# Hybrid decoder trunk: how the weight pairs of the feed-forward block are brought in, and how its output tiles are added to the residual

## The chip, the cores and the metric

The kernel runs on one core of one Trainium2 chip. The metric is device time in microseconds (us) for one execution. The five engines are TensorE (PE for its matmuls, PEld for its weight loads), VectorE (DVE), ScalarE (ACT), GpSimd (POOL) and SyncE (SP). Transfers are issued by an engine's queue in the order of that engine's program and carried out by 16 DMA engines that all queues share. An instruction whose input is not there holds up everything behind it on its own engine.

## The reference, cut to what matters

Two layers over 512 tokens with a width of 1024. Each layer has three token mixers (attention in a window, a short convolution, a state space model), merged by gates, and then a feed-forward block with a hidden width of 2816; a final RMSNorm ends it. The change touches the feed-forward block only:

```
h = rmsnorm(x, norm_ffn[i])
gt, up = jnp.split(h @ w_ffn_in[i], 2, axis=-1)
x = x + (jax.nn.silu(gt) * up) @ w_ffn_out[i]
```

Everything is float32. A float32 product is made of three matmuls on split operands: each operand is a high part `h` (the value rounded to fp32r) and a low part `l` (the value less `h`), and the product is hh + lh + hl.

## The kernel before, in words

**Tiles.** Activations lie transposed, 128 channels by 512 tokens to a tile. A weight chunk is fetched as a raw tile, ACT copies it to `h` with rounding (`A.copy`), DVE subtracts to get `l` (`lo_of`), and PE uses both.

**The pairs.** The hidden width is cut into 22 tiles of 128, in the groups 0-5, 6-9, 10-13, 14-17 and 18-21. The first six tiles are plain. From tile 6 on, the gate tile and the up tile of a hidden tile make a *pair*, which is computed with seven products of half-sized blocks in place of eight (`seven_products`). A pair item needs the four blocks a11, a12, a21, a22 of its weights, two sums of them and a copy of one, each split into `h` and `l`. The groups 6-9, 10-13 and 14-17 are also multiplied by the output weights in this way (`out_pairs`): two pair items for each group, each used for four of the eight output tiles. Their results are added to the residual, which is kept in DRAM in `xkept`. A layer has 22 pair items: 16 for hidden tiles and 6 for out pairs. The out pairs of a group come behind the first hidden tile of the next group, so the items are, from 0: tiles 6, 7, 8, 9, 10, then out pairs (items 5 and 6), tiles 11 to 14, out pairs (11 and 12), tiles 15 to 18, out pairs (17 and 18), tiles 19 to 21. This stretch is called the pair stretch below. Group 18-21 is multiplied out plainly at its end (`pfo`).

**How a pair item is brought in.** `fetch_chunk` issues for each item, on POOL's queue: r2 = (a21, a11) (L175); h4 = a22, rounded to fp32r by the transfer (L176); then (a22, a21) accumulated onto r2 by a transfer (L177), which has to wait until the first load of r2 has landed; and r1 = (a11, a12) (L178). `item_steps` then lets ACT write -h4 into l4 (L195) and a transfer on POOL's queue accumulate a22 onto it (L196). DVE makes r3 from r2 and r1 (L225, L227); ACT makes h1, h2, h3 (L223, L230, L234) and DVE l1, l2, l3 (L190).

**How an output tile is stored.** For each pair of output tiles `out_pairs` loads both residual tiles from `xkept` ahead (L1184, tiles `xs`), adds the products on DVE and stores each tile back (L1189, L1193), all on SP's queue.

**What sets the order.** The program is traced in the order of the code and then put into an order for each engine by a scheduler that works on a timeline of its own. Buffers are handed out in that order: r1, r2 and r3 share 5 buffers, `h` and `l` of weights have 5 each, and 58 buffers of 128x512 (pool `u2`) hold all the rest, h4, l4, `xs`, ga and ub among them. A transfer or an operation that writes a buffer waits until the last use of its previous content is over.

Of the kernel before, what the change touches and what calls it, by code (L numbers as in the profile page):

```python
# [9 lines left out]
F32 = mybir.dt.float32  # L10
F32R = mybir.dt.float32r
I32 = mybir.dt.int32
AF = mybir.ActivationFunctionType
ALU = mybir.AluOpType
PSUM = bass.MemoryType.PSUM

P = 128
D = 1024
S = 512
DEPTH = 2  # L20
KT = D // P
# [59 lines left out]
def hybrid_kernel(ctx, tc, xin, wst, wsp, vec, ssp, ssb, sbt, cst, out):  # L81
    nc = tc.nc
    V, A, T = nc.vector, nc.scalar, nc.tensor
# [13 lines left out]
    def u2(shape, dt=F32, name="u2"):  # L97
        return up.tile(shape, dt, tag="u2", bufs=NU2, name=name)
# [58 lines left out]
    raws = []  # L157

    def wraw(name, dt=F32):
        return wp.tile([P, 1024], dt, tag="part", bufs=NPART, name=name)  # L160

    def whi(name="whi", dt=F32R):
        return wp.tile([P, 1024], dt, tag="whi", bufs=NHI, name=name)

    def wlo(name="wlo", dt=F32R):
        return wp.tile([P, 1024], dt, tag="wlo", bufs=NLO, name=name)

    def fetch_chunk(queue=nc.sync, parts=1):
        i, n, *half = items[loaded[0]]
        loaded[0] += 1  # L170
        if n is None:

            r1, r2, h4 = wraw("r1"), wraw("r2"), u2([P, S], F32R, "h4")
            n = half[0]
            nc.gpsimd.dma_start(r2[:, : 2 * n], wsp[i, :, 1024 : 1024 + 2 * n])  # L175
            nc.gpsimd.dma_start(h4[:, :n], wsp[i, :, 2048 : 2048 + n])  # L176
            nc.gpsimd.dma_start(r2[:, : 2 * n], wsp[i, :, 2048 : 2048 + 2 * n], accum_op=ALU.add)  # L177
            nc.gpsimd.dma_start(r1[:, : 2 * n], wsp[i, :, 0 : 2 * n])  # L178
            raws.append((i, n, r1, r2, h4))
            return None  # L180
        raw = wp.tile([P, 1024], F32, tag="raw", bufs=NRAW, name="raw")
        n //= parts
        cuts = [slice(j * n, (j + 1) * n) for j in range(parts)]
        for c in cuts:
            dma = queue.dma_start(raw[:, c], wst[i, :, c])
        raws.append((raw, cuts))
        return dma

    def lo_of(lo, raw, hi):
        V.tensor_tensor(out=lo, in0=raw, in1=hi.bitcast(F32), op=ALU.subtract)  # L190
        return lo

    def rest_of(lo, hi, src):

        A.activation(lo, hi.bitcast(F32), AF.Copy, scale=-1.0)  # L195
        nc.gpsimd.dma_start(lo, src, accum_op=ALU.add)  # L196
        return lo

    fetched = [0]
# [1 line left out]
    def item_steps():  # L201
        if not raws:
            fetch_chunk()
        got = raws.pop(0)
        while sum(1 + (len(x) > 3) for x in raws) < fetched[0] and loaded[0] < len(items):
            fetch_chunk()
        if len(got) == 2:
            raw, cuts = got
            hi, lo = whi(), wlo()
            for c in cuts:  # L210
                A.copy(hi[:, c], raw[:, c])  # L211
                yield
                lo_of(lo[:, c], raw[:, c], hi[:, c])
                yield
            ready.append((cuts[-1].stop * 3 // P, (hi, lo)))
            return
        i, n, r1, r2, h4 = got
        a, b, ab = slice(0, n), slice(n, 2 * n), slice(0, 2 * n)
        l4 = u2([P, S], F32R, "l4")
        rest_of(l4[:, a], h4[:, a], wsp[i, :, 2048 : 2048 + n])  # L220
        yield
        h1 = whi("h1")
        A.copy(h1[:, ab], r1[:, ab])  # L223
        r3 = wraw("r3")
        V.tensor_tensor(out=r3[:, a], in0=r2[:, a], in1=r1[:, a], op=ALU.add)  # L225
        yield
        V.tensor_tensor(out=r3[:, b], in0=r3[:, a], in1=r1[:, b], op=ALU.add)  # L227
        yield
        h2, l1 = whi("h2"), wlo("l1")
        A.copy(h2[:, ab], r2[:, ab])  # L230
        lo_of(l1[:, ab], r1[:, ab], h1[:, ab])
        yield
        h3, l2 = whi("h3"), wlo("l2")
        A.copy(h3[:, ab], r3[:, ab])  # L234
        lo_of(l2[:, ab], r2[:, ab], h2[:, ab])
        yield
        l3 = wlo("l3")
        lo_of(l3[:, ab], r3[:, ab], h3[:, ab])
        part = lambda h, l, c: (h[:, c], l[:, c])
        ready.append((7 * n // P * 3 // 2,  # L240
            dict(a11=part(h1, l1, a), a12=part(h1, l1, b), s1=part(h2, l2, a), s3=part(h2, l2, b),
                 s2=part(h3, l3, a), s4=part(h3, l3, b), a22=part(h4, l4, a))
        ))
        yield

    def load_chunk():
        for _ in item_steps():
            pass
# [3 lines left out]
    def feed(steps=1000):  # L252

        while steps and sum(n for n, _ in ready) < AHEAD and (feeding or raws or loaded[0] < len(items)):
            if not feeding:
                feeding.append(item_steps())
            if next(feeding[0], "end") == "end":
                feeding.pop()
            steps -= 1

    def take():
        while not ready:
            feed(1)
        return ready.pop(0)[1]
# [97 lines left out]
    def tt(out, a, b, op):  # L362
        V.tensor_tensor(out=out, in0=a, in1=b, op=op)
        return out

    def stt(out, a, s, b, o0, o1):
        V.scalar_tensor_tensor(out=out, in0=a, scalar=s, in1=b, op0=o0, op1=o1)
        return out
# [10 lines left out]
    for k in range(KT):  # L379
# [3 lines left out]
        if k == 3:  # L383
            fetch_chunk()
    xg = []
    first = item_steps()
    with tc.manual_schedule(engines={mybir.EngineType.DVE, mybir.EngineType.Activation}):
        for k in range(KT):
# [63 lines left out]
    def first_products(ssum):  # L452

        u = u_products(ssum)
        pq, ws = [mmps([P, S], "pqb") for _ in range(NB - 1)], [chunk()]
        q_products(pq, ws, [0], range(NB - 1))
        u = u_evacuated(*u)
        ws.append(chunk())
        q_products(pq, ws, [1], range(NB - 1))
        pq.append(mmps([P, S], "pqb"))  # L460
        q_products(pq, ws, [0, 1], [NB - 1])
        return u + ((pq, ws),)
# [5 lines left out]
    uts, rcol, rb, r2, qprod = first_products(ssum)  # L468
# [16 lines left out]
    def tiny(dt=F32, shape=(P, LQ)):  # L485
        _n[0] += 1
        return cp.tile(list(shape), dt, name=f"ssm_c{_n[0]}")
# [73 lines left out]
    for lo_, hi_, by in ((2, 3, 1), (3, 5, 2)):  # L561
        n = hi_ - lo_
        dst = [pw[:, i, lo_:hi_] for i in range(2)]
        src = [pw[:, i, lo_ - by : hi_ - by] for i in range(2)]
        m = [pw[:, i, by : by + 1].to_broadcast([P, n, LQ]) for i in range(2)]
# [27 lines left out]
    r4 = er  # L593
    for _ in range(2):
        cph, sph = double_angle(cph, sph)
        r4 = tt(tiny(), r4, r4, ALU.mult)
# [324 lines left out]
    for l in range(DEPTH):  # L921
        if l > 0:
            uts, rcol, rb, r2, qprod = first_products(ssum)
# [204 lines left out]
        flat = lambda x: x.rearrange("p a c -> p (a c)")  # L1128
# [34 lines left out]
        def pair_tile(made, beside):  # L1163

            ga, ub, pd, pb = seven_products(ops, beside, take())

            def evacuated():
                tt(ga, ga, pd, ALU.add)
                A.activation(ga, ga, AF.Silu)
                yield  # L1170
                stt(ub, pb, -1.0, ub, ALU.mult, ALU.subtract)
                yield
                yield from made(flat(ga), flat(ub))

            return [evacuated()]

        def out_pairs(ops, beside):

            xs = []

            def fetch_x(m):
                xs.append([u2([P, S], F32, "xs") for _ in range(2)])
                for j in range(2):
                    nc.sync.dma_start(xs[-1][j], xkept[:, m + j])  # L1184

            def evacuated(m, x, ga, ub, pd, pb):
                tt(ga, ga, pd, ALU.add)
                tt(x[0], x[0], flat(ga), ALU.add)
                nc.sync.dma_start(xkept[:, m], x[0])  # L1189
                yield  # L1190
                stt(ub, pb, -1.0, ub, ALU.mult, ALU.subtract)
                tt(x[1], x[1], flat(ub), ALU.add)
                nc.sync.dma_start(xkept[:, m + 1], x[1])  # L1193
                yield

            fetch_x(0)
            for m in range(0, KT, 2):
                if m + 2 < KT:
                    fetch_x(m + 2)
                if m % 4 == 0:  # L1200
                    w = take()
                got = seven_products(ops, beside, w, m % 4)
                beside = [evacuated(m, xs.pop(0), *got)]
            return beside

        xkept = dr.tile([P, KT, S], F32, name=f"xkept{l}")
        nonlocal_rb = []
        beside, due = [], []
        for gi, (f0, f1) in enumerate(FGROUPS):
# [14 lines left out]
            for f in range(f0, f1):  # L1224
# [12 lines left out]
                beside = pair_tile(made, beside)  # L1237
                if due:
                    beside = out_pairs(due.pop(), beside)
# [6 lines left out]
            beside = []  # L1246
# [238 lines left out]
```

## Time and profile before

| | |
|---|---|
| time, median of 3 runs | 1584.59 us (1581.96 to 1584.94) |
| profiled execution, its own time | 1581.27 us |
| its span | 1579.3 us |
| PE busy | 1544.9 us (98% of the span) |
| DVE, ACT, POOL busy | 1172.7, 731.1, 268.1 us |
| moved by DMA | 245.89 MB |
| pair stretch, layer 0 and layer 1 | about 536 to 761 us, about 1311 to 1531 us |

Rows of the profile give the line, the engine, the operation, the tile written and the tiles read (buffer numbers left out, so r1, r2 and r3 are all `r`). In groups, the numbers behind the bar are the busy time, the mean duration in ns, and then the idle time of that engine just before these instructions, with what ended it. In a timeline each row has the start, the length, and in brackets the idle time before it and its releaser. The releaser is inferred: where the engine named had long been done, it was another, often a transfer. The lines "issue to landing" give the median from the issue of a transfer until its data has arrived.

### The profile page before, as it was taken

How to read it: one execution, taken by the hardware profiler on the slowest of the kernel's cores; microseconds unless marked ns; L12 is line 12 of the kernel's file. 1: busy time of each engine (PE TensorE's matmuls, PEld its weight loads, DVE VectorE, ACT ScalarE, POOL GpSimd, SP SyncE). 2: the span in 40 equal slices, each digit the busy share in tenths (PEclk: the TensorE clock that was granted, in tenths of full speed). 3: DMA queues.
4: the chain of work that ended last, by engine and by line, in shares of the span. 5: the costliest groups of instructions: out<-in, count | busy, mean ns of one | idle time of the engine just before them, and what ended most of it. 6: DMA issues, size and time to landing. Idle time of an engine off the chain costs nothing.

```text
span 1579.3 us, 24934 instructions
## 1 busy us (share of the span) xinstructions
PE 1544.9 (98%) x9204; PEld 1351.1 (86%) x9204; DVE 1172.7 (74%) x2294; ACT 731.1 (46%) x1314; POOL 268.1 (17%) x451
## 2 busy tenths in 40 slices
PE   9899999999999999999999999999999999999996
PEld 7777878888888999999888778788888889999995
DVE  7985869766667687988768666896476756888876
ACT  4345533334444365665524555233444434665652
POOL 0301023210001133332020012122100012333201
PEclk9999999999999999999999999999999999999998
DMA  6423235432533899989543233345234258999952
GB/s 224 124 82 81 78 94 136 137 107 89 179 100 96 227 223 273 280 235 255 188 140 114 74 84 89 115 111 157 73 126 160 84 161 215 252 253 287 271 166 89
DMA packets 108026, 245.89 MB, mean 156 GB/s; under 512 B 23072, under 2 KB 28480, under 8 KB 107904
## 3 DMA queue, kind: packets, MB, share of 16 engines
q1 hardware_dynamic: 69280, 144.77, 28.0%
q0 software_dynamic: 38336, 99.00, 25.7%
q8 instruction: 73, 1.20, 0.3%
q10 hardware_dynamic: 288, 0.52, 0.1%
q14 instruction: 49, 0.40, 0.1%
HBM read 218.01 MB, written 22.02 MB: 152 GB/s over the span
## 4 chain that ended last, share of the span: by engine, by line
PE 82%; DMA 6%; DVE 5%; issue 4%; ACT 1%; POOL 1%; SPq 0%; DVEq 0%; POOLq 0%; ACTq 0%
PE pg L275 17%; PE pc L275 11%; PE py L275 8%; PE pd L275 7%; PE pfo L275 7%; PE pb L275 7%; PE px L275 6%; PE pfu L275 4%; PE pfg L275 4%; DMA r<-wsp 3%; DMA xkept<-xs 2%; PE pu L275 1%; PE pqb L275 1%; PE pz L275 1%; PE pS L857 1%
## 5 line engine op out<-in xcount | busy, mean ns | idle before, releaser
L211 ACT CAST whi<-raw 128x1024 fp32r<-128x1024 f32 (+2 forms) x214 | 195.4, 917 | 434.2 <-PE pg L275 114.2
L190 DVE TENSOR_TENSOR wlo<-raw,whi 128x1024 fp32r<-128x1024 f32 (+2 forms) x214 | 225.4, 1055 | 93.9 <-ACT whi L211 82.3
L190 DVE TENSOR_TENSOR l<-r,h 128x1024 fp32r<-128x1024 f32 x132 | 160.4, 1218 | 12.5 <-ACT h L234 10.5
L275 PE MATMUL pg<-hi,whi 128*128 128x512 f32 x384 | 152.2, 396 | 0.0
L275 PE MATMUL pg<-hi,wlo 128*128 128x512 f32 x384 | 150.4, 392 | 0.0
L275 PE MATMUL pg<-lo,whi 128*128 128x512 f32 x384 | 150.0, 391 | 0.0
L275 PE MATMUL pd<-hi,l 128*128 128x256 f32 x528 | 148.1, 283 | 1.7 <-DVE l L190 1.7
L275 PE MATMUL pd<-hi,h 128*128 128x256 f32 x528 | 148.3, 283 | 0.0
L275 PE MATMUL pd<-lo,h 128*128 128x256 f32 x528 | 147.9, 283 | 0.0
L275 PE MATMUL pb<-hi,h 128*128 128x256 f32 x352 | 100.5, 285 | 6.9 <-ACT ga L1148 5.5
L275 PEld LDWEIGHTS pd<-hi,l 128*128 128x128 f32 x528 | 100.9, 192 | 2.1 <-DVE l L190 2.1
L275 PEld LDWEIGHTS pd<-lo,h 128*128 128x128 f32 x528 | 100.9, 192 | 0.0
L275 PEld LDWEIGHTS pd<-hi,h 128*128 128x128 f32 x528 | 100.9, 192 | 0.0
L275 PE MATMUL pb<-hi,l 128*128 128x256 f32 x352 | 99.6, 283 | 0.0
L275 PE MATMUL pb<-lo,h 128*128 128x256 f32 x352 | 99.6, 283 | 0.0
L176 POOL DMA_DIRECT2D h<-wsp x44 | 29.6, 674 | 362.4 <-PE pfu L275 330.6
L275 PEld LDWEIGHTS pg<-hi,whi 128*128 128x128 f32 x384 | 72.2, 188 | 15.8 <-DVE at_nm L357 0.4
L275 PEld LDWEIGHTS pg<-hi,wlo 128*128 128x128 f32 x384 | 72.1, 188 | 15.2
L275 PEld LDWEIGHTS pg<-lo,whi 128*128 128x128 f32 x384 | 72.2, 188 | 14.3
L275 PE MATMUL pc<-hi,whi 128*128 128x512 f32 x192 | 77.9, 406 | 2.4 <-ACT qr L820 2.4
L275 PE MATMUL pc<-lo,whi 128*128 128x512 f32 x192 | 76.5, 399 | 0.0
L275 PE MATMUL pc<-hi,wlo 128*128 128x512 f32 x192 | 76.3, 397 | 0.0
(302 smaller groups left out, 4327.6 us busy)
## 6 DMA issues: line engine op xcount, KB each, us to landing
raw<-wst SPq DMA_DIRECT2D x140, 512.0 KB, 3.5
r<-wsp POOLq DMA_DIRECT2D x132, 512.0 KB, 6.5
raw<-wst SPq DMA_DIRECT2D x56, 256.0 KB, 2.7
xs<-xkept SPq DMA_DIRECT2D x48, 256.0 KB, 6.1
xkept<-xs SPq DMA_DIRECT2D x48, 256.0 KB, 6.4
h<-wsp POOLq DMA_DIRECT2D x44, 256.0 KB, 5.8
l<-wsp POOLq DMA_DIRECT2D x44, 256.0 KB, 7.3
raw<-wst SPq DMA_DIRECT2D x16, 384.0 KB, 3.0
```

The lines of the kernel that those rows point to most:

```text
L176: nc.gpsimd.dma_start(h4[:, :n], wsp[i, :, 2048 : 2048 + n])
L190: V.tensor_tensor(out=lo, in0=raw, in1=hi.bitcast(F32), op=ALU.subtract)
L211: A.copy(hi[:, c], raw[:, c])
L275: T.matmul(o, a, b, start=start and i == 0, stop=stop and i == 2, skip_group_check=more)
L857: T.matmul(pS[par][:, hp, keys], qt[a][rows, 2 * k + hp], kt[b][rows, k, keys], start=i == 0, stop=i == 2,)
```

## The change

Three things change, for both layers.

1. The plain loads of a pair item (r2, r1) go to SP's queue. The accumulation onto r2 stays on POOL's queue and waits for the load on the other queue.
2. The fourth block is loaded as raw float32 (r4) on SP's queue; ACT rounds it to h4 and DVE subtracts to get l4, as for the other blocks. The second read of a22 and the accumulation onto l4 are gone.
3. The output tiles of the out pairs are no longer loaded, added on DVE and stored. Each product tile (ga, ub) is accumulated onto its tile of `xkept` in DRAM by one transfer on POOL's queue.

```diff
-            r1, r2, h4 = wraw("r1"), wraw("r2"), u2([P, S], F32R, "h4")
+            r1, r2, r4 = wraw("r1"), wraw("r2"), u2([P, S], F32, "r4")
             n = half[0]
-            nc.gpsimd.dma_start(r2[:, : 2 * n], wsp[i, :, 1024 : 1024 + 2 * n])
-            nc.gpsimd.dma_start(h4[:, :n], wsp[i, :, 2048 : 2048 + n])
+            nc.sync.dma_start(r2[:, : 2 * n], wsp[i, :, 1024 : 1024 + 2 * n])
             nc.gpsimd.dma_start(r2[:, : 2 * n], wsp[i, :, 2048 : 2048 + 2 * n], accum_op=ALU.add)
-            nc.gpsimd.dma_start(r1[:, : 2 * n], wsp[i, :, 0 : 2 * n])
-            raws.append((i, n, r1, r2, h4))
+            nc.sync.dma_start(r1[:, : 2 * n], wsp[i, :, 0 : 2 * n])
+            nc.sync.dma_start(r4[:, :n], wsp[i, :, 2048 : 2048 + n])
+            raws.append((i, n, r1, r2, r4))
...
-    def rest_of(lo, hi, src):
-
-        A.activation(lo, hi.bitcast(F32), AF.Copy, scale=-1.0)
-        nc.gpsimd.dma_start(lo, src, accum_op=ALU.add)
-        return lo
...
-        l4 = u2([P, S], F32R, "l4")
-        rest_of(l4[:, a], h4[:, a], wsp[i, :, 2048 : 2048 + n])
-        yield
...
+        yield
+        h4, l4 = u2([P, S], F32R, "h4"), u2([P, S], F32R, "l4")
+        A.copy(h4[:, a], r4[:, a])
+        lo_of(l4[:, a], r4[:, a], h4[:, a])
         yield
         l3 = wlo("l3")
...
-            def evacuated(m, x, ga, ub, pd, pb):
+            def evacuated(m, ga, ub, pd, pb):
                 tt(ga, ga, pd, ALU.add)
-                tt(x[0], x[0], flat(ga), ALU.add)
-                nc.sync.dma_start(xkept[:, m], x[0])
+                nc.gpsimd.dma_start(xkept[:, m], flat(ga), accum_op=ALU.add)
                 yield
                 stt(ub, pb, -1.0, ub, ALU.mult, ALU.subtract)
-                tt(x[1], x[1], flat(ub), ALU.add)
-                nc.sync.dma_start(xkept[:, m + 1], x[1])
+                nc.gpsimd.dma_start(xkept[:, m + 1], flat(ub), accum_op=ALU.add)
                 yield
 
-            fetch_x(0)
             for m in range(0, KT, 2):
-                if m + 2 < KT:
-                    fetch_x(m + 2)
                 if m % 4 == 0:
                     w = take()
                 got = seven_products(ops, beside, w, m % 4)
-                beside = [evacuated(m, xs.pop(0), *got)]
+                beside = [evacuated(m, *got)]
```

The line numbers of the changed kernel are lower by up to 17. Three places show how its instructions stand.

**POOL, first out pairs of layer 0.** The numbers count buffers in the order in which the program makes them: r2_5860 and r1_5859 are item 8 (tile 12), r2_6006 and h4_6007 item 9 (tile 13), r2_6151 and h4_6152 item 10 (tile 14), h4_6275 is item 11. Before:

```order
L175 DMA r2_5860<-wsp 128x1024
L176 DMA h4_5861<-wsp 128x512
L196 DMA l4_5866<-wsp 128x512
L178 DMA r1_5859<-wsp 128x1024
L177 DMA r2_5860<-wsp 128x1024
L176 DMA h4_6007<-wsp 128x512
L196 DMA l4_6012<-wsp 128x512
L175 DMA r2_6006<-wsp 128x1024
L178 DMA r1_6005<-wsp 128x1024
L176 DMA h4_6152<-wsp 128x512
L196 DMA l4_6157<-wsp 128x512
L177 DMA r2_6006<-wsp 128x1024
```

After, with item 8 as r2_5859, item 9 as r2_5995, item 10 as r2_6137 and item 11 as r2_6260:

```order
L176 DMA r2_5859<-wsp 128x1024
L1176 DMA xkept0_4365<-ga_5848 128x512
L1179 DMA xkept0_4365<-ub_5849 128x512
L1176 DMA xkept0_4365<-ga_5929 128x512
L1179 DMA xkept0_4365<-ub_5930 128x512
L176 DMA r2_5995<-wsp 128x1024
L1176 DMA xkept0_4365<-ga_5984 128x512
L1179 DMA xkept0_4365<-ub_5985 128x512
L1176 DMA xkept0_4365<-ga_6065 128x512
L1179 DMA xkept0_4365<-ub_6066 128x512
L176 DMA r2_6137<-wsp 128x1024
L176 DMA r2_6260<-wsp 128x1024
```

POOL's queue now holds accumulations only: item 9's stands behind those of the first four output tiles, item 10's behind all eight.

**SP, the same place.** Before, SP carried the residual tiles; after, the loads of items 8 to 11.

```order
L1184 DMA xs_5838<-xkept0_4365 128x512
L1184 DMA xs_5839<-xkept0_4365 128x512
L1184 DMA xs_5842<-xkept0_4365 128x512
L1184 DMA xs_5843<-xkept0_4365 128x512
L1184 DMA xs_5926<-xkept0_4365 128x512
L1184 DMA xs_5927<-xkept0_4365 128x512
L1189 DMA xkept0_4365<-xs_5838 128x512
L1184 DMA xs_5987<-xkept0_4365 128x512
L1193 DMA xkept0_4365<-xs_5839 128x512
```

```order
L175 DMA r2_5859<-wsp 128x1024
L178 DMA r4_5860<-wsp 128x512
L177 DMA r1_5858<-wsp 128x1024
L178 DMA r4_5996<-wsp 128x512
L175 DMA r2_5995<-wsp 128x1024
L178 DMA r4_6138<-wsp 128x512
L177 DMA r1_5994<-wsp 128x1024
L175 DMA r2_6137<-wsp 128x1024
L178 DMA r4_6261<-wsp 128x512
L177 DMA r1_6136<-wsp 128x1024
```

The r4 of the next item stands ahead of the loads of an item, and nothing but these loads stands on SP here.

**DVE, the second half of the same out pairs.** Before, and then after:

```order
L225 TENSOR_TENSOR r3_6027<-r2_5860,r1_5859 128x512
L227 TENSOR_TENSOR r3_6027<-r3_6027,r1_5859 128x512
L363 TENSOR_TENSOR ga_5994<-ga_5994,pd_5993 128x512
L363 TENSOR_TENSOR xs_5926<-xs_5926,ga_5994 128x512
L367 SCALAR_TENSOR_TENSOR ub_5995<-pb_5991,ub_5995 128x512
L363 TENSOR_TENSOR ga_6076<-ga_6076,pd_6075 128x512
L363 TENSOR_TENSOR xs_5927<-xs_5927,ub_5995 128x512
L363 TENSOR_TENSOR xs_5987<-xs_5987,ga_6076 128x512
L190 TENSOR_TENSOR l1_6037<-r1_5859,h1_6025 128x1024
```

```order
L358 TENSOR_TENSOR ga_5984<-ga_5984,pd_5983 128x512
L216 TENSOR_TENSOR r3_6003<-r2_5859,r1_5858 128x512
L218 TENSOR_TENSOR r3_6003<-r3_6003,r1_5858 128x512
L362 SCALAR_TENSOR_TENSOR ub_5985<-pb_5981,ub_5985 128x512
L358 TENSOR_TENSOR ga_6065<-ga_6065,pd_6064 128x512
L190 TENSOR_TENSOR l1_6016<-r1_5858,h1_6001 128x1024
L190 TENSOR_TENSOR l4_6184<-r4_5996,h4_6183 128x512
L362 SCALAR_TENSOR_TENSOR ub_6066<-pb_6062,ub_6066 128x512
```

The additions into `xs` are gone, and one subtraction for l4 has come in for each item. Ahead of the feed-forward block the orders of PE, DVE and ACT are the same in both kernels; there only the loads of items 0 and 1 stand elsewhere, on SP among the raw chunks instead of on POOL.

More of the change, by code (lines that the diff above doesn't have):

```diff
@@ L216, in item_steps @@
             return
-        i, n, r1, r2, h4 = got
+        i, n, r1, r2, r4 = got
         a, b, ab = slice(0, n), slice(n, 2 * n), slice(0, 2 * n)
-        l4 = u2([P, S], F32R, "l4")
-        rest_of(l4[:, a], h4[:, a], wsp[i, :, 2048 : 2048 + n])
-        yield
         h1 = whi("h1")
@@ L1177, in out_pairs @@
         def out_pairs(ops, beside):
[L1179 to L1184, printed above, removed]
-            def evacuated(m, x, ga, ub, pd, pb):
+            def evacuated(m, ga, ub, pd, pb):
                 tt(ga, ga, pd, ALU.add)
-                tt(x[0], x[0], flat(ga), ALU.add)
-                nc.sync.dma_start(xkept[:, m], x[0])
+                nc.gpsimd.dma_start(xkept[:, m], flat(ga), accum_op=ALU.add)
                 yield
                 stt(ub, pb, -1.0, ub, ALU.mult, ALU.subtract)
-                tt(x[1], x[1], flat(ub), ALU.add)
-                nc.sync.dma_start(xkept[:, m + 1], x[1])
+                nc.gpsimd.dma_start(xkept[:, m + 1], flat(ub), accum_op=ALU.add)
                 yield
-            fetch_x(0)
             for m in range(0, KT, 2):
-                if m + 2 < KT:
-                    fetch_x(m + 2)
                 if m % 4 == 0:
```

## Prediction

> **What bounds the kernel now.** I read the page's first part and the chain of waits first, then the busy time by stretches, then who PE waits for, then the timelines around the longest of these waits.
>
> ```profile
> span 1579.3 us, 24934 instructions
> PE 1544.9 (98%) x9204; PEld 1351.1 (86%) x9204; DVE 1172.7 (74%) x2294; ACT 731.1 (46%) x1314; POOL 268.1 (17%) x451
> PE 82%; DMA 6%; DVE 5%; issue 4%; ACT 1%; POOL 1%; SPq 0%; DVEq 0%; POOLq 0%; ACTq 0%
> ```
>
> PE is busy for all but 34.4 us. The chain still puts 6% on transfers: PE is the bound, but in places the chain runs beside PE and nearly as late. How much of PE's idle time lies in the pair stretches, the only place that the change touches, is told by windows (PE's busy time stands after the length):
>
> ```profile
> 586.00:611.00 25.00, 25.00 (x210) 25.00 (x210) 22.20 (x31) 15.08 (x29) 8.71 (x13) 1.00 1.05 292
> 611.00:641.00 30.00, 28.95 (x241) 28.75 (x240) 23.70 (x34) 17.40 (x31) 8.76 (x13) 1.00 0.89 239
> 641.00:671.00 30.00, 30.00 (x252) 30.00 (x251) 27.53 (x40) 18.56 (x38) 10.12 (x15) 1.00 1.04 303
> 671.00:701.00 30.00, 27.79 (x232) 27.59 (x231) 22.14 (x31) 15.90 (x27) 8.76 (x13) 1.00 0.94 250
> sum 225.00, PE 220.07 PEld 219.06 DVE 182.21 ACT 133.07 POOL 63.33; mean PE 36.68 PEld 36.51 DVE 30.37 ACT 22.18 POOL 10.55
> sum 220.00, PE 216.38 PEld 215.36 DVE 180.10 ACT 129.92 POOL 63.11; mean PE 54.09 PEld 53.84 DVE 45.02 ACT 32.48 POOL 15.78
> ```
>
> The two sums are the stretches of layer 0 and layer 1: 4.93 + 3.62 = 8.55 us idle. That is all the change can win there, apart from a little pipeline refill. PE isn't idle in the out pairs (586 to 611), where the DMA share is over 1, but in the 30 us behind them. Who it waits for there:
>
> ```profile
> PE pb L275 <- ACT ga L1148: 5.5, 6, 2.2
> PE pd L275 <- DVE l L190: 1.7, 2, 0.8
> PE pb L275 <- ACT ga L1153: 1.4, 2, 0.8
> PE pfo L275 <- DVE xres L363: 0.5, 1, 0.5
> DVE r L225 <- DMA r<-wsp: 35.3, 12, 5.4
> POOL r L177 <- DMA r<-wsp: 140.3, 39, 7.8
> ```
>
> The first three add up to these 8.6 us. ACT's copies are not the cause; the second half of the rows shows a late r2. The longest case (POOL, then DVE, ACT, PE):
>
> ```profile
> 675.29 0.88 POOL L175 DMA_DIRECT2D r<-wsp  x1
> 684.91 0.88 POOL L177 DMA_DIRECT2D r<-wsp  x1 [8.19 <-DVE ga L363]
> 691.17 0.69 DVE L225 TENSOR_TENSOR r<-r,r 128x512 f32<-128x512 f32 x1 [5.43 <-DMA r<-wsp]
> 692.50 0.68 DVE L363 TENSOR_TENSOR ga<-ga,pd 128x512 f32<-128x512 f32 x1
> 693.22 0.63 ACT L1169 ACTIVATE ga<-ga 128x512 f32<-128x512 f32 x1 [5.11 <-DVE ga L363]
> 694.69 0.36 ACT L1148 COPY ga<-pb 128x256 f32<-128x256 f32 x1
> 695.11 0.39 PE L275 MATMUL pb<-hi,h 128*128 128x256 f32 x1 [2.21 <-ACT ga L1148]
> ```
>
> r2 is loaded at 675.29, accumulated onto at 684.91 and ready at 691.17, 15.9 us later. DVE stands before r3; behind it in DVE's order is the ga that ACT's Silu needs, behind that on ACT the copy that frees the PSUM bank, and for that PE waits 2.21 us. In a quiet part the same two steps begin 5.3 us apart:
>
> ```profile
> 547.26 0.54 POOL L175 DMA_DIRECT2D r<-wsp  x1 [2.91 <-DVE l L190]
> 552.53 0.88 POOL L177 DMA_DIRECT2D r<-wsp  x1 [2.46 <-DMA r<-wsp]
> ```
>
> **The change part by part.** *Bytes.*
>
> ```profile
> r<-wsp POOLq DMA_DIRECT2D x132, 512.0 KB, 6.5
> raw<-wst SPq DMA_DIRECT2D x140, 512.0 KB, 3.5
> xs<-xkept SPq DMA_DIRECT2D x48, 256.0 KB, 6.1
> xkept<-xs SPq DMA_DIRECT2D x48, 256.0 KB, 6.4
> l<-wsp POOLq DMA_DIRECT2D x44, 256.0 KB, 7.3
> 537.50 2.88 PE pd L275 x24
> ```
>
> From the last row a matmul takes 0.12 us, so an item of 84 (seven products, four blocks, three matmuls) lasts 10.08 us and the out pairs of a group two items, 20.16 us. An item brings 2048 KB now (3 x 512, 2 x 256) and 1792 KB after. In out pairs 8 residual tiles are read and 8 written as well: 2 x 2048 + 16 x 256 = 8192 KB in 20.16 us, 416 GB/s, against the 292 GB/s in the row 586 to 611. So the work spills over into what follows, and that is where r2 is late. After, it is 2 x 1792 + 8 x 256 = 5632 KB, or 7680 KB if the tile that an accumulation reads counts as well: 286 to 390 GB/s.
>
> *Time until r2 is ready.* An item is split while PE works on the one before it, since only then buffers for its `h` and `l` come free; its r buffers then go to the item after the next. So item 4 could load when item 2 was split, just after item 1 began, and it did: counted from 536 us at 10.08 us each, item 1 began at 546.1, the load at 547.26. In the same count item 10 (tile 14) may load about 2 us into item 7, at 608.6, and is wanted when item 8 ends, at 626.7. With 6.5 us for the load and 6.5 us for the accumulation (the median of both kinds together) it is ready near 622, 4 to 5 us in time. Before, POOL's order put item 9's accumulation, two h4 and two l4 ahead of this load. On SP only r4 and r1 stand ahead.
>
> POOL's own new waits: item 9's accumulation stands behind the accumulation of four output tiles, the last of which is due about 1.5 us after the first half of the out pairs, near 598, when r2 is still on its way until about 605 (two us into item 6, and 6.5). Item 10's stands behind all eight, due near 608, its load landing near 615. Both waits are hidden by the load itself. Priced without that cover: 6.5 us late for an item whose reserve is 4 to 5 us, so 2 us of PE for each of six out pairs.
>
> *Engines.*
>
> ```profile
> L190 DVE TENSOR_TENSOR wlo<-raw,whi 128x512 fp32r<-128x512 f32 x58 | 39.7, 685 | 17.9 <-ACT whi L211 12.9 <-DMA pt<-pfd 4.8
> L363 DVE TENSOR_TENSOR xs<-xs,ga 128x512 f32<-128x512 f32 x24 | 16.5, 688 | 0.4
> L363 DVE TENSOR_TENSOR xs<-xs,ub 128x512 f32<-128x512 f32 x24 | 16.4, 684 | 0.1
> L195 ACT ACTIVATE l<-h 128x512 fp32r<-128x512 f32 x44 | 27.5, 633 | 6.0 <-PE pb L275 4.0 <-DMA h<-wsp 0.8 <-DMA xkept<-xs 0.5
> L289 ACT CAST hi<-t 128x512 fp32r<-128x512 f32 x40 | 24.7, 618 | 21.9 <-DVE t L367 21.7
> L196 POOL DMA_DIRECT2D l<-wsp x44 | 42.4, 975 | 33.9 <-ACT l L195 17.9 <-DVE lo L290 11.1 <-ACT ga L1148 1.7
> ```
>
> DVE loses 16.5 + 16.4 = 32.9 us in the out pairs and gains 44 x 0.685 = 30.1 us over all items: the 20.16 us of out pairs lose 8 x 0.69 and gain 2 x 0.69, 4.1 us less of a load of 22.20 in 25. A tile's 10.08 us take 0.69 more: of the fullest row above, 27.53 of 30, it would be 27.53 + 2.1 = 29.6 of 30, were there no `xs` in it, and there is some. Rows overlap by about 0.08 us each, so true room is left, but thin. ACT's rounding costs 0.62 in place of 0.63 us: nothing. POOL exchanges four issues per item for one accumulation per output tile, and was busy 8.71 of 25 us: no term.
>
> *Ahead of the pairs*, the loads of items 0 and 1 now stand on SP, where a wait would hold up raw chunks.
>
> ```profile
> 240.91 0.57 POOL L175 DMA_DIRECT2D r<-wsp  x1 [25.08 <-PE py L767]
> 236.74 13.11 SPq L185 DMA_DIRECT2D raw<-wst  x3
> 241.31 8.54 SPq L185 DMA_DIRECT2D raw<-wst  x2
> ```
>
> The first load's buffer came free at 240.91; on SP it stands between the chunk that went out at 236.74 and the one at 241.31: it costs nothing. Out of step by as much as its 25.08 us, it would starve PE of chunks for about 20 us.
>
> *The sum.* Of the 8.55 us, the six waits on L1148 and two on L1153 (6.9 us) come from the late r2 or from a buffer held by a residual tile's store; I take 80% of them as gone, 5.5 us. The two on `l` (1.7 us) sit behind `xs` additions on DVE: half, 0.8 us. Refill and the wait on `xres`: 0.7 us. Against it 1 us of new small waits on a fuller DVE. Net 6.0 us. Bounds: all 8.55 + 0.5 and some 2 us refill, about 11, on one side; no gain and 3 us of new waits on the other. On the profiled execution 1581.27 - 6.0 = 1575.3; that execution lies 3.3 us under the median of the runs, 1584.59, so the forecast is 1578.6.
>
> **The rivals.** *A: the transfers are the bound, not their order.* The moved loads then land no earlier, the tile that an accumulation reads counts (7680 of 8192 KB), and only a fourth of the gain is left: 1.5 us, 1583. For it speaks the DMA share of 1.05; against it, that POOL's L177 waited 140.3 us in all with loads queued behind it. [...]
>
> *B: DVE.* The 0.69 us more for each of 32 tiles puts ga or a weight's `l` late: 0.2 us for each tile would cost 6.4 us and cancel the gain: 1584 to 1585. Against it: all PE waits behind `l` in both layers are 1.7 us.
>
> *C: slower, by held buffers.* ga and ub are now free only when their accumulation has landed. The ub of the last step of the out pairs takes the buffer of the first ga, about 10 us after its accumulation is issued, and so do the next tile's ga and ub in turn. Stores to `xkept` land in 6.4 us and accumulations of that size in 7.3; under 10 nothing happens. If reading and writing DRAM makes 13 us, each of six out pairs loses 3 us: 18 - 6 = 12 us slower, 1597. From about 11 us on the gain is gone. [...]
>
> **How the numbers follow.** The forecast has 0.56, A 0.18, B 0.10, C 0.13, and a load on SP that holds up the chunks 0.03 (1600). About 0.2% (3.2 us) can be told from no change. Faster by more: the forecast's 0.56 and 0.02 of A, 0.58. Same: the rest of A, and B, 0.26. Slower: C and the last, 0.16. The forecast's own range is 1573 to 1582 (gains of 11 to 3); A and B reach 1586, and up to 1588 a weak C. I give 1571 to 1588.
>
> **What would show it.** Right: the wait of PE's pb on ACT's ga falls from 5.5 to under 1.5 us, that of DVE's r on transfers from 35.3 to under 10, and PE's idle time in the two stretches from 8.55 to 2 or 3 us; accumulations to `xkept` land within 10 us; bytes fall by 24 MB less what accumulations read. Wrong: PE waits on `l` grow over 4 us (B), ACT's ga or ub waits on accumulations into `xkept` (C), SP waits in front of r2 while raw chunks are late.

## The result, and the profile after

| | before | after |
|---|---|---|
| device time, median of 6 runs each | 1582.82 us (1578.82 to 1584.94) | 1574.01 us (1572.59 to 1576.11) |
| profiled execution | 1581.27 us | 1572.64 us |
| its span | 1579.3 us | 1570.9 us |

The ratio is 0.995, with a 95% interval of 0.9933 to 0.9966: 8.8 us, or 0.5%, faster. The forecast was 6.0 us faster. The page of the changed kernel, its first part, the chain of waits and the two large DMA queues (packets, MB, share of 16 engines' span):

```profile
span 1570.9 us, 24730 instructions
PE 1542.7 (98%) x9204; PEld 1349.6 (86%) x9204; DVE 1171.5 (75%) x2290; ACT 730.4 (46%) x1314; POOL 198.3 (13%) x323
q1 hardware_dynamic: 74464, 177.28, 35.2%
q0 software_dynamic: 19904, 42.37, 15.9%
PE 89%; DMA 5%; DVE 3%; ACT 1%; issue 1%; SPq 0%; DVEq 0%; POOLq 0%; ACTq 0%
```

The same two queues of the kernel before:

```profile
q1 hardware_dynamic: 69280, 144.77, 28.0%
q0 software_dynamic: 38336, 99.00, 25.7%
```

PE has 82% of the chain before and 89% after, so more of the end is set by PE itself. Bytes fell by 24.15 MB (10%, 245.89 to 221.74), but the time of the transfers hardly did: (28.0 + 25.7)% of 1579.3 us are 848 us, (35.2 + 15.9)% of 1570.9 are 803 us, 5%. The two queues moved bytes at different rates. After, POOL's queue (q0), which now carries accumulations for 35.7 of its 42.4 MB, moved these 42.37 MB in 250 us, 170 GB/s; SyncE's (q1) before 144.77 MB in 442 us, 327 GB/s.

The pair stretches after, in windows from the first `pb` matmul to the last group's output (PE's busy time stands after the length):

```profile
536.70:757.00 220.30, 219.43 (x1826) 219.02 (x1825) 180.77 (x246) 133.34 (x238) 37.04 (x43) 1.00 0.83 195
1305.80:1527.00 221.20, 218.17 (x1816) 217.76 (x1815) 179.58 (x245) 132.78 (x236) 36.90 (x43) 1.00 0.82 191
```

PE's idle time there is 0.87 + 3.03 = 3.9 us, against 8.55. What PE and DVE still wait for (line 1143 copies `pb`, as line 1148 did before; line 216 is `r3`):

```profile
PE pb L270 <- ACT ga L1143: 3.9, 4, 2.8
PE pfo L270 <- DVE xres L358: 0.9, 1, 0.9
PE pfo L270 <- ACT hi L284: 1.1, 1, 1.1
DVE r L216 <- DMA r<-wsp: 23.2, 4, 7.6
```

The waits on `l` (1.7 us) and on line 1153 (1.4 us) are gone. The late r2 is not: DVE waits 4 times in place of 12, but longer each time. The longest of the four, in the chain of waits (start, length, what):

```profile
1440.91 6.53 DMA r<-wsp
...
1448.07 12.63 DMA r<-wsp
...
1460.78 0.70 DVE r L216
```

r2's load lands in 6.53 us, its accumulation takes 12.63, and PE waits 2.78 us behind it. On POOL's queue four accumulations of output tiles, issued from 1440.29 to 1442.57 us, stand ahead of this one, and the last of them lands at 1457.16. The issues, with the median time to landing:

```profile
r<-wsp SPq DMA_DIRECT2D x88, 512.0 KB, 4.8
r<-wsp POOLq DMA_DIRECT2D x44, 512.0 KB, 6.1
xkept<-ga POOLq DMA_DIRECT2D x24, 256.0 KB, 7.5
xkept<-ub POOLq DMA_DIRECT2D x24, 256.0 KB, 8.5
```

**Where the 8.5 us between the two profiled executions went**, by the first matmul of each stage in the two traces. +0.8 in the first 150 us, which the change doesn't touch. -4.9 in the pair stretch of layer 0 (225.1 to 220.2 us) and -1.4 in that of layer 1 (223.8 to 222.4). +0.4 between the layers. And -3.3 from the last output products to the end (46.0 to 42.7), of which the prediction's sum had only the wait on `xres` (0.5 us before, 0.9 after): before, PE waited 2.2 us there on ACT's `hi`, and then ran at half its clock for 3.4 us (last section); after, it waited 1.1 us and the clock stayed. Whether the change brings this about or it fell so in these two executions was not tested.

### The profile page after: what moved, and what is told of

Same layout as the page of the kernel before. It is cut to its first block, busy times and chain, and to the rows that moved or that the text cites. A ratio compares the mean times of both kernels' runs of the same rounds, so it can differ in the third digit from the quotient of the medians.

```text
span 1570.9 us, 24730 instructions
## 1 busy us (share of the span) xinstructions
PE 1542.7 (98%) x9204; PEld 1349.6 (86%) x9204; DVE 1171.5 (75%) x2290; ACT 730.4 (46%) x1314; POOL 198.3 (13%) x323
## 2 busy tenths in 40 slices
DMA packets 94776, 221.74 MB, mean 141 GB/s; under 512 B 21600, under 2 KB 27008, under 8 KB 94656
## 3 DMA queue, kind: packets, MB, share of 16 engines
q1 hardware_dynamic: 74464, 177.28, 35.2%
q0 software_dynamic: 19904, 42.37, 15.9%
## 4 chain that ended last, share of the span: by engine, by line
PE 89%; DMA 5%; DVE 3%; ACT 1%; issue 1%; SPq 0%; DVEq 0%; POOLq 0%; ACTq 0%
PE pg L270 17%; PE pc L270 11%; PE pb L270 10%; PE pd L270 9%; PE py L270 8%; PE pfo L270 6%; PE px L270 6%; DMA r<-wsp 4%; PE pfu L270 4%; PE pfg L270 4%; PE pu L270 3%; PE pqb L270 2%; PE pz L270 1%; PE pS L852 1%; PE po L898 1%; PE pvv L736 1%
## 5 line engine op out<-in xcount | busy, mean ns | idle before, releaser
L190 DVE TENSOR_TENSOR l<-r,h 128x1024 fp32r<-128x1024 f32 (+1 forms) x176 | 187.9, 1086 | 11.1 <-ACT h L214 4.7
L176 POOL DMA_DIRECT2D r<-wsp x44 | 38.0, 863 | 731.9 <-DMA r<-wsp 491.6
```

## The experiments

In all of them S stands for the plain loads on SyncE's queue, R for the fourth block split on chip, X for the accumulation of output tiles; the change is S + R + X. Ratios are to the kernel before, run on the same chip; its medians there were 1583.6 to 1586.3 us. Some expectations give PE's idle time in the pair stretches as 10 us for the kernel before, 4.5 for the changed one and 1.05 for R + X. By the rows of the profile it is 8.55, 3.9 and 0.9, about 0.15 us less for each wait.

**S alone.**

```diff
-            nc.gpsimd.dma_start(r2[:, : 2 * n], wsp[i, :, 1024 : 1024 + 2 * n])
+            nc.sync.dma_start(r2[:, : 2 * n], wsp[i, :, 1024 : 1024 + 2 * n])
...
-            nc.gpsimd.dma_start(r1[:, : 2 * n], wsp[i, :, 0 : 2 * n])
+            nc.sync.dma_start(r1[:, : 2 * n], wsp[i, :, 0 : 2 * n])
```

> The kernel before with one part of the change: the two plain 512 KB loads of an item (r2, r1) go on SyncE's queue, h4, both accumulations and the residual tiles stay as they were. Theory of order (the prediction's): r2 was late because its load stood on POOL behind accumulations and h4; so this part alone takes PE's idle time in the two pair stretches from 8.55 to about 3 us, and the time from 1582.8 to about 1577. Theory of transfer time (a rival formed from the trace after): an accumulating transfer moves about 170 GB/s where a plain one moves 320, so that counted in plain KB an item cost 512+512+256+2x512+2x256 = 2816 before and 512+512+256+2x512 = 2304 after, whatever queue it is on; the order alone gives next to nothing: idle time 7 to 9 us, time 1581 to 1583.

Measured: 1594.42 us, ratio 1.0055 (1.0037 to 1.0073): 8 us slower. Neither theory had that. PE's waits:

```profile
PE pb L275 <- ACT ga L1148: 9.7, 4, 3.3
PE pb L275 <- ACT ga L1153: 3.7, 2, 1.9
```

The accumulations of r2 (line 177, in the pair stretches) before:

```profile
DMA to landing us min/median/max: 5.3/6.4/8.8
```

and with S alone:

```profile
DMA to landing us min/median/max: 5.4/7.3/10.4
```

The loads left POOL's queue, and the accumulation that stayed there became slower.

**R alone**, all loads on POOL: `r4` in place of `h4`, copied and split by ACT and DVE as in the change.

```diff
-            nc.gpsimd.dma_start(h4[:, :n], wsp[i, :, 2048 : 2048 + n])
+            nc.gpsimd.dma_start(r4[:, :n], wsp[i, :, 2048 : 2048 + n])
...
-            rest_of(l4[:, a], h4[:, a], wsp[i, :, 2048 : 2048 + n])
+            A.copy(h4[:, a], r4[:, a])
+            lo_of(l4[:, a], r4[:, a], h4[:, a])
```

> The kernel before with one part of the change: the fourth block is loaded once (r4, plainly) and split by ACT and DVE; all loads stay on POOL's queue, the residual tiles go through xs as before. Theory of order: only one h4 less ahead of r2's load and no l4, so at most 2 us less: idle time 6.5 to 8.5 us, time 1581 to 1583. Theory of transfer time: the item falls from 2816 to 2304 plain KB (18%), which is most of what the change saves: idle time 3 to 5 us, time 1577 to 1579.

Measured: 1575.77 us, ratio 0.9936 (0.992 to 0.9953). The two queues and DVE's wait before `r3`:

```profile
q1 hardware_dynamic: 69280, 144.77, 28.3%
q0 software_dynamic: 29184, 87.46, 21.9%
DVE r L216 <- DMA r<-wsp: 6.0, 5, 2.6
```

Transfers take 50.2% of 1575.0 us, 791 us against 848, and DVE's wait for r2 falls from 35.3 to 6.0 us, though nothing was put on another queue. One part, the one that takes transfer time away, gives at least as much as the whole change. But it also takes the accumulation of line 196, with 33.9 us of idle time on POOL before it, out of POOL's line, and puts the load of the fourth block behind the others; no run separates this from the transfer time. That less transfer time in the same order is enough for a gain of this size (0.5%), the plain load in place of r2's accumulation shows below.

**X alone**, weights as before.

```diff
-                tt(x[0], x[0], flat(ga), ALU.add)
-                nc.sync.dma_start(xkept[:, m], x[0])
+                nc.gpsimd.dma_start(xkept[:, m], flat(ga), accum_op=ALU.add)
```

> The kernel before with one part of the change: output tiles are accumulated onto the residual in DRAM on POOL's queue, weights are loaded as before, all on POOL. Theory of order: eight accumulations now stand on POOL among the loads of r2, each waiting for DVE, so r2 comes later or at the same time: idle time 8 to 12 us, time 1583 to 1586. Theory of transfer time: an accumulation of 256 KB takes as much as a read and a store apart (4096 plain KB for an out pair before and after), so nothing from the transfers, and a little from 33 us less on DVE: idle time 7 to 9 us, time 1581 to 1583.

Measured: 1577.23 us, ratio 0.9948 (0.993 to 0.9965), better than either theory.

```profile
q0 software_dynamic: 45248, 111.58, 30.3%
q1 hardware_dynamic: 55456, 119.60, 23.4%
```

53.7% of 1578.0 us are 847 us: the transfers take as long as before, as the theory of transfer time had it, though the trace's bytes fell by 12.6 MB. The gain is not in the time of the transfers.

**R + X**, the changed kernel with its plain loads put back on POOL.

```diff
-            nc.sync.dma_start(r2[:, : 2 * n], wsp[i, :, 1024 : 1024 + 2 * n])
+            nc.gpsimd.dma_start(r2[:, : 2 * n], wsp[i, :, 1024 : 1024 + 2 * n])
...
-            nc.sync.dma_start(r1[:, : 2 * n], wsp[i, :, 0 : 2 * n])
-            nc.sync.dma_start(r4[:, :n], wsp[i, :, 2048 : 2048 + n])
+            nc.gpsimd.dma_start(r1[:, : 2 * n], wsp[i, :, 0 : 2 * n])
+            nc.gpsimd.dma_start(r4[:, :n], wsp[i, :, 2048 : 2048 + n])
```

> The changed kernel with its three plain loads of an item put back on POOL's queue (fourth block split on chip, output tiles accumulated in DRAM). Theory of order: loads wait on POOL behind accumulations of output tiles that wait for DVE, so most of the gain goes: idle time 6 to 10 us, time 1579 to 1583. Theory of transfer time: the same transfers as in the changed kernel, so the same time within 0.1%: 1573 to 1576, idle time about 5 us.

Measured: 1570.83 us, ratio 0.9908 (0.9891 to 0.9924), below the interval of the whole change (0.9933 to 0.9966). It is faster than the kernel before and the changed one. PE has nothing left to lose in layer 1's pair stretch (219.00 us long):

```profile
1305.00:1524.00 219.00, 218.99 (x1825) 218.79 (x1824) 180.48 (x246) 133.64 (x238) 67.76 (x98) 1.00 0.81 194
```

So S costs 0.55% on the kernel before and, as the ratio of two ratios, 0.995 / 0.9908, 0.42% here (each of the two with an interval of about 0.17% to either side): 7 to 9 us. Why, was the next question.

**S + R**, the change without X (residual tiles as before).

> The changed kernel without the accumulation onto the residual (xs loads, DVE additions and stores as before): plain loads on SyncE's queue and the fourth block split on chip. Theory of two queues (formed from the runs of single parts): plain loads on SyncE's queue no longer stand in line behind POOL's accumulations but share the transfer engines with them, so that the accumulation on which r3 waits lands later; then the move costs here too, some 4 to 8 us against the same kernel with the loads on POOL (1575.8): 1580 to 1584, accumulations of r2 landing in 6.5 to 7.5 us at the median. Theory that the move only hurts in company (with l4's accumulations, or with those of output tiles, on POOL): no loss, 1574 to 1577.

Measured: 1583.94 us, ratio 0.9995 (0.9979 to 1.0011): S takes back all that R gives (0.9995 / 0.9936, 0.59%). The accumulations of r2 land in 6.3 us at the median, a little under what was expected; here the trace shows another road for the cost. ACT's row of the longest case in its timeline, and PE's behind it:

```profile
727.30 0.37 ACT L1143 COPY ga<-pb 128x256 f32<-128x256 f32 x1 [3.41 <-DMA xkept<-xs]
...
727.72 0.39 PE L270 MATMUL pb<-hi,h 128*128 128x256 f32 x1 [3.84 <-ACT ga L1143]
```

The residual tiles' loads and stores are on SyncE's queue too, and now stand among the weights. ACT waits for a store to give a buffer back, and PE for ACT. With X there are no such stores.

**R + X with r1 alone on SyncE**, and **with r2's load alone there.**

```diff
-            nc.gpsimd.dma_start(r1[:, : 2 * n], wsp[i, :, 0 : 2 * n])
+            nc.sync.dma_start(r1[:, : 2 * n], wsp[i, :, 0 : 2 * n])
```

> The fastest kernel so far (fourth block split on chip, output tiles accumulated, all loads on POOL: 1570.8) with one 512 KB load of an item, r1, put on SyncE's queue. r1 is issued behind r2's accumulation on POOL; on SyncE it runs beside it. Theory of two queues: the accumulation of r2 lands later (slowest over 10 us, against 8.0), idle time of PE in the pair stretches 2 to 4 us against 1.05, time 1572 to 1575. If the loss comes from r2's own load on SyncE: no change, 1569 to 1572.

> The fastest kernel so far (1570.8) with r2's plain load alone put on SyncE's queue, r1 and r4 on POOL. Theory of two queues: this load runs beside the accumulations of output tiles and of the item before it, and lands earlier than on POOL in the out pairs, but its accumulation still stands in line behind those of the output tiles on POOL; what the load takes from them comes back as a later accumulation: 1 to 3 us of idle time in the pair stretches, 1571 to 1574. The prediction's theory (r2's load is late because of its place on POOL's queue): a gain of up to the 1.05 us that is left, 1569 to 1571.

Measured: with r1 there 1579.02 us, ratio 0.9971 (0.9956 to 0.9985); with r2 there 1569.71, ratio 0.9909 (0.989 to 0.9929). r1 does the harm, by itself 0.6%, and r2 does none. Not quite as expected: the accumulations are no slower (7.5 us at most). It is r2's plain load that comes late. With r1 on SyncE, the issues of one item in the first out pairs (612.06 and 612.44 us):

```profile
r<-wsp POOLq DMA_DIRECT2D x1, 512.0 KB, 11.3
r<-wsp SPq DMA_DIRECT2D x1, 512.0 KB, 6.9
```

and POOL's timeline there (r2's load, its accumulation):

```profile
612.06 1.54 POOL L175 DMA_DIRECT2D r<-wsp  x1
...
623.61 0.88 POOL L176 DMA_DIRECT2D r<-wsp  x1 [8.55 <-DMA r<-wsp]
```

r1, issued 0.4 us behind r2, lands 4.0 us ahead of it. On POOL's queue the accumulations issued at 610.97 and 611.52 us and then r2 landed in that order, at 620.3, 621.9 and 623.4; r1, on SyncE's queue, landed ahead of all three, at 619.3. The accumulation onto r2 can only start at 623.61, and PE waits 3.92 us. The same item with all on POOL:

```profile
610.61 1.89 POOL L175 DMA_DIRECT2D r<-wsp  x1
...
612.63 1.89 POOL L177 DMA_DIRECT2D r<-wsp  x1
620.29 0.88 POOL L176 DMA_DIRECT2D r<-wsp  x1 [5.78 <-DMA r<-wsp]
```

Here r1 (line 177) queues behind r2 and lands behind it, the accumulation starts 9.7 us after the load in place of 11.6, and PE doesn't wait. With all on POOL's queue, the transfers issued from 610.06 to 612.63 us landed in the order of their issue, from 618.5 to 622.8, and the last accumulation ahead of r2 and r2 itself took 8.4 and 9.1 us; with r1 on SyncE's queue these two took 10.4 and 11.3. In the changed kernel it is the accumulation itself that comes last: issued at 1448.07 (the 12.63 us above), it landed at 1460.70, after the loads of r2 and r1 issued at 1449.12 and 1450.85 on SyncE's queue, which landed at 1457.13 and 1459.35. r4 alone on SyncE's queue was not run.

**The change with r2's accumulation as a plain load** (the sum of two blocks is left out, so its values are not the reference's).

```diff
-            nc.gpsimd.dma_start(r2[:, : 2 * n], wsp[i, :, 2048 : 2048 + 2 * n], accum_op=ALU.add)
+            nc.gpsimd.dma_start(r2[:, : 2 * n], wsp[i, :, 2048 : 2048 + 2 * n])
```

> The changed kernel with r2's accumulation replaced by a plain load of the same 512 KB on the same queue at the same place (the sum of the two blocks is left out, so its values are not the reference's). An item then costs 512 x 3 + 256 = 1792 plain KB in place of 2304. Theory of two queues: with no slow transfer on POOL but those of the output tiles the step lands in 4 to 5.5 us instead of 6.1 (slowest under 10 against 12.6), idle time in the pair stretches falls from 4.5 us to about 1, time 1569 to 1572. If the loss is in waiting for issue (SyncE or POOL blocked by a wait), the kind of transfer makes no difference: 1573 to 1576.

Measured: 1568.08 us, ratio 0.9899 (0.9878 to 0.992); the step lands in 4.7 us at the median and 7.8 at most, and no PE wait over 0.3 us is left in the pair stretches.

```profile
q0 software_dynamic: 19904, 42.37, 11.8%
```

The same packets and bytes took 185 us in place of 250. The 44 transfers of 512 KB are 23.07 MB; at the 327 GB/s of plain ones they would take 71 us, and accumulating costs 65 more: by this estimate 1.9 times a plain load. With that gone, PE shows no harm from S, although the accumulations of output tiles are still on POOL's queue: it is r2's accumulation beside it that makes S costly.

**The kernel before with r2's load alone on SyncE**, the prediction's central step by itself.

```diff
-            nc.gpsimd.dma_start(r2[:, : 2 * n], wsp[i, :, 1024 : 1024 + 2 * n])
+            nc.sync.dma_start(r2[:, : 2 * n], wsp[i, :, 1024 : 1024 + 2 * n])
```

> The kernel before with one line moved: r2's plain load on SyncE's queue; r1, h4 and both accumulations stay on POOL. This is the prediction's central step alone (r2's load taken out of POOL's line). The prediction's theory: nearly the whole gain of the order, idle time of PE in the pair stretches from 10 to 3 or 4 us, 1577 to 1580. Theory of two queues: which transfer gets ahead decides; r2 gets ahead of r1, h4 and l4 here, so it gains too, but the accumulations behind it are as slow as before and share the engines with it: a part of it, 1579 to 1584. If any load on SyncE harms this kernel: 1588 or more, like the kernel with r2 and r1 there (1594).

Measured: 1585.2 us, ratio 1.0007 (0.9991 to 1.0023): nothing.

```profile
PE pb L275 <- ACT ga L1148: 5.6, 4, 1.8
PE pb L275 <- ACT ga L1153: 1.9, 1, 1.9
PE pb L275 <- DVE l L190: 1.6, 1, 1.6
DVE r L225 <- DMA r<-wsp: 33.8, 9, 8.2
```

DVE waits as long for r2 as before (35.3), and new waits stand beside the old ones.

**R + X with r2's accumulation as additions on GpSimd**, the loads on POOL's queue, and **the same with the loads on SyncE's.**

```diff
-            nc.gpsimd.dma_start(r2[:, : 2 * n], wsp[i, :, 2048 : 2048 + 2 * n], accum_op=ALU.add)
+            nc.gpsimd.dma_start(r4[:, :n], wsp[i, :, 2048 : 2048 + n])
+            nc.gpsimd.dma_start(r5[:, :n], wsp[i, :, 2048 + n : 2048 + 2 * n])
+            nc.gpsimd.tensor_tensor(out=r2[:, :n], in0=r2[:, :n], in1=r4[:, :n], op=ALU.add)
+            nc.gpsimd.tensor_tensor(out=r2[:, n : 2 * n], in0=r2[:, n : 2 * n], in1=r5[:, :n], op=ALU.add)
```

> The fastest kernel so far (1570.8; all loads on POOL) with r2's accumulation by transfer replaced by two additions on GpSimd: the two halves of the third part are loaded plainly (one of them is the fourth block, so r4 is not loaded again) and added onto r2. Transfer time of an item: 1536 plain KB in place of 2304. If transfers are all that is left: idle time in the pair stretches from 1.05 to 0, 1568 to 1571. If GpSimd's additions (0.71 us for 128x256 in the trace before, so some 2.9 us an item) hold up the issues behind them or slow DVE's operations: 1574 to 1584, to be seen in DVE's mean times (0.685 us for 128x512).

> The same with the plain loads on SyncE's queue as in the change, so that POOL's queue holds only the accumulations onto the residual, and the additions. Theory of two queues: with 1536 plain KB an item and no accumulation of r2, sharing the engines costs next to nothing: like the kernel with all on POOL, within 2 us. If SyncE's queue harms by itself (its order, or its waits): 4 us or more slower than that.

Measured: 1584.08 us, ratio 1.001 (0.9997 to 1.0023), and 1583.72, ratio 0.9994 (0.9978 to 1.001). All of R + X's gain is gone, wherever the loads are: with no accumulation of r2, SyncE's queue costs nothing here. The traces point to DVE, whose sums for `r3` (0.905 us on average in place of 0.690) and subtractions for `l` (1.368 in place of 1.220) became slower, and in the first of the two PE waits 4.6 us on `l`, which it doesn't in R + X; how much of the loss this makes is not shown. With the loads on POOL:

```profile
L193 DVE TENSOR_TENSOR l<-r,h 128x1024 fp32r<-128x1024 f32 x132 | 179.8, 1368 | 12.7 <-ACT h L228 10.8 <-ACT h L217 1.3 <-ACT h L224 0.4
L219 DVE TENSOR_TENSOR r<-r,r 128x512 f32<-128x512 f32 x44 | 39.8, 905 | 17.6 <-DMA r<-wsp 16.3
L179 POOL TENSOR_TENSOR r<-r,r 128x512 f32<-128x512 f32 x44 | 83.4, 1896 | 99.4 <-DMA r<-wsp 99.4
```

The same two DVE groups in R + X:

```profile
L190 DVE TENSOR_TENSOR l<-r,h 128x1024 fp32r<-128x1024 f32 x132 | 160.3, 1220 | 9.2 <-ACT h L214 4.0 <-ACT h L225 3.3 <-ACT h L221 1.4
L216 DVE TENSOR_TENSOR r<-r,r 128x512 f32<-128x512 f32 x44 | 30.3, 690 | 35.2 <-DMA r<-wsp 28.4 <-PE py L760 4.1 <-issue 1.2
```

**X alone, with DVE's load put back**: an operation of the size of the residual addition ahead of each accumulation.

```diff
+                tt(flat(ga), flat(ga), flat(ga), ALU.max)
                 nc.gpsimd.dma_start(xkept[:, m], flat(ga), accum_op=ALU.add)
```

> The kernel before with output tiles accumulated onto the residual in DRAM (alone, this gave 1577.2), and on DVE, ahead of each accumulation, one operation of the same size as the residual addition that it replaced (the maximum of a tile with itself, 128x512, which leaves it as it is). It tells where the accumulation's gain comes from. If from DVE (33 us of additions gone, behind which l and ga were late): the gain goes, 1582 to 1586, and PE's two waits of 0.84 us on l (line 190) in the third group are back. If from buffers, held no longer by residual tiles and their stores: most of it stays, 1576 to 1580, and the waits on l stay away.

Measured: 1575.3 us, ratio 0.9952 (0.9937 to 0.9967), as X alone, and the waits on `l` stay away. X's gain is not DVE's. By elimination it is left with the residual tiles, their loads and stores and the buffers that these hold; before, ACT's copies waited 3.4 us for such stores, with S + R 7.4 us on line 1143 alone. How much of the 8 us each of these makes was not measured.

## Why the prediction was right, and where it was wrong

The time and its sign were right, and 1574.0 lies in the forecast's own range, near its fast end. The forecast was counted from 1584.59 us; the six runs of the kernel before have 1582.82, so a gain of 6.0 us stands against 8.8. The reason was right in part: PE lost its time in the pair stretches, to an r2 that came late because too much had to be moved around the out pairs. The steps:

- **"So the work spills over"** held, but it was sized in bytes. What spills is transfer time. Counting an accumulating KB as 1.9 plain ones, or 2 in round numbers, an item is 2816 KB before and 2304 after (18% less), not 2048 and 1792 (12%); and an out pair's residual traffic is 16 x 256 plain KB before and 8 x 256 accumulated ones after, the same.
- **"On SP only r4 and r1 stand ahead"** is the step that failed. The move off POOL's queue was to bring nearly all of the 5.5 us. By itself it costs 8 us, in the change 7. r2's load alone on SyncE's queue gives nothing (ratio 1.0007). The step looked at the order of issue alone. The gain of 5.5 us was put down mostly to S and came with R and X (ratios 0.9936 and 0.9948 alone). The 6.5 us for an accumulation were too few as well where four of output tiles stand ahead of it: 12.63 us in the longest case, with the load at 6.53. The sum counted when those four would be issued, and not the time that they take on the queue.
- **X** was priced only through bytes and DVE: "The two on l (1.7 us) sit behind xs additions on DVE: half". They went altogether, but not because of DVE's load (with that load put back they stay away), and X alone is worth 8 us. The stores that hold buffers were named and lumped into the 5.5 us.
- **"That is all the change can win there"** looked at the pair stretches; behind them, in the last output products, there was 1.1 us less waiting on ACT's `hi` and no slow clock. The wait on `xres`, counted as gone, grew from 0.5 to 0.9 us, and the pipeline refill was 0.1 us behind each wait (the second matmul starts 0.22 us after the first, in place of 0.12): with 10 such waits before and 4 after, 0.6 us of gain by this estimate, against 0.2 in the sum and 2 in the bounds.
- The 1 us of new waits from a fuller DVE was not seen: no wait of PE on `l` is left, and DVE is busy 180.77 of 220.30 us in layer 0's stretch.

The sum came out near by luck, because two errors cancelled: S, booked as most of the gain, costs 7 us, and R and X together give 15 us (0.92%) where the whole sum had 6.

Of the rivals, **A** had the mechanism: the tile that an accumulation reads counts, in time though not in the trace's bytes, and loads on SyncE do not land free. Its price was wrong, since it counted the accumulations of weights by their bytes: 7680 of 8192 KB in an out pair, 6% less, where at twice the price it is 8704 of 9728, 11% less. **B** did not come: no wait on `l`. **C** had a landing time for which it was to decide, 11 us, and such landings happened (up to 14.6 us for an `ub`), with two waits of ACT on them after, 0.4 us together; in X alone three, 2.1 us. That xs tiles no longer take buffers from the same pool may be the reason; it was not tried. Of the signs, the bytes (24.15 MB fewer) came as expected, and the accumulations onto the residual landed within the 10 us given for them at the median (7.5 and 8.5) but not all (up to 14.6); PE's idle time was 3.9 us (2 to 3 expected), the wait on `ga` 3.9 (under 1.5), DVE's wait for r2 23.2 (under 10). The last two said that r2 was still late although the time was met.

## What to carry to other kernels

Price a transfer in engine time, not in bytes: read it from the share of each queue (here 170 GB/s on the queue that mostly accumulated, 327 on the plain one). Before a load is moved to a second queue, ask who then loses its place. Here the order of issue on one queue protected the transfer that the path waits for, a load with a slow accumulation behind it (9.7 us from one to the other), and with r1 on a second queue what was less urgent landed ahead of it (11.6 us, and PE waited 3.92). And undo the parts of a change one by one even when the whole is a gain: here one of three parts cost half of what the other two gave.

## What the runs showed of the hardware that was not expected

**PE's clock fell to half on a fixed grid.** The granted clock in all fourteen traces changes only at steps of 3.41 us. Two places, in windows laid on this grid; the kernel before, behind its wait at the last output products:

```profile
1540.00:1543.41 3.41, 1.22 (x11) 1.02 (x9) 2.73 (x4) 0.87 (x2) 0.00 (x0) 1.00 0.98 338
1543.41:1546.83 3.42, 3.42 (x17) 3.23 (x17) 2.18 (x6) 1.67 (x4) 0.00 (x0) 0.50 0.13 49
```

and the changed kernel at its longer wait:

```profile
1460.07:1463.48 3.41, 1.87 (x16) 1.66 (x14) 2.66 (x4) 0.65 (x2) 0.00 (x0) 1.00 0.74 141
1463.48:1466.90 3.42, 2.18 (x18) 2.18 (x19) 3.42 (x6) 3.42 (x7) 0.00 (x0) 1.00 0.55 150
```

A wait of 2.19 us within one step was followed by a step at 0.50, in which matmuls of 128x256 began every 0.21 us in place of 0.12: about 1.5 us of the 3.42, by this estimate; one of 2.78 us that fell across two steps (1.54 and 1.24 us) was not. Over the fourteen traces, from 15 to 1553 us, with PE's idle time counted in gaps over 0.3 us: all 19 steps with 1.9 us or more were followed by half the clock, of 8 with 1.6 to 1.9 us four were, and of 52 with 1.2 to 1.6 us none. In the kernel before, the steps from 65.44 and 1540.00 us, with 2.23 and 2.19 us idle, were followed by 0.50, and the one from 693.50, with 1.61, by 1.00. (The ends of matmuls are modelled, so these limits may be off by some 0.2 us.) So the price of a wait of 2 to 3 us depends on where it falls, which may be part of why six runs of the kernel before lie 6.1 us apart and six of R + X, with hardly a long wait, 3.9 (1568.94 to 1572.81).

**With additions on GpSimd, some of DVE's operations took longer.** With additions of 1.9 and 1.7 us on GpSimd and the loads on POOL's queue, DVE's two sums for `r3` take 0.905 and 0.959 us on average in place of 0.690, and its sum of `ga` and `ub` 0.783 in place of 0.686, while its sum of `ga` and the product `pd` takes 0.679 against 0.685. What makes the difference between them was not shown.
